# Rope's half swap in an attention stage: GpSimd's products replaced by transfers between partitions and one VectorE product

## The chip, the core and the metric

The kernel runs on one core of one Trainium2 chip. The metric is the device time of one execution in microseconds (us), the median of three runs. TensorE (PE) multiplies matrices, VectorE (DVE), ScalarE (ACT) and GpSimd (POOL) work on tiles of up to 128 partitions, SyncE (SP) issues the transfers of the weights.

## What is computed

Two transformer layers with expert lookup and one hybrid block on 256 tokens of width 1024, in float32. The change lies in the first layer's attention alone: eight heads, each with two query and key maps of width 64 whose softmaxes are subtracted. Its part of the reference:

```python
def _rope(t, cos, sin):
    half = t.shape[-1] // 2
    rot = jnp.concatenate([-t[..., half:], t[..., :half]], axis=-1)
    return (t * cos[None, :, None, :] + rot * sin[None, :, None, :]).astype(t.dtype)
...
    q = _rope(q.reshape(B, S, 2 * DIFF_HEADS, DIFF_HEAD_DIM), cos, sin)
    k = _rope(k.reshape(B, S, 2 * DIFF_HEADS, DIFF_HEAD_DIM), cos, sin)
...
    scale = DIFF_HEAD_DIM ** -0.5
...
        s = jnp.einsum('bhmqd,bhmkd->bhmqk', qblk, kh).astype(jnp.float32) * scale
        p = jax.nn.softmax(jnp.where(mask, s, -jnp.inf), axis=-1)
        a = p[:, :, 0] - lam * p[:, :, 1]
        return jnp.einsum('bhqk,bhkd->bhqd', a.astype(vh.dtype), vh)
```

## The kernel before

Every weight is streamed from memory in tiles of 128 × 1024 (`Stream`, lines 36 to 85): SP loads a tile raw, ACT copies it to hi (line 66), DVE subtracts it to lo (line 67), and a product becomes three matmuls, with hi, with lo, and with the low part of the activations (lines 157 to 159). There are four raw buffers and three pairs of parts; splits run two tiles ahead of use.

`layer0` (line 366) does the first layer's attention. `proj_half` (line 209) makes the first half of v, then `qk_head` (line 509) makes q and k of one head after the other: a projection (`proj_t`, 24 matmuls of 256 columns), `rope`, a tick. At the end come the second half of v, the output projection (`proj_n`) and the layer norm.

q and k of a head stand transposed: 128 partitions are two maps of 64, each two halves of 32, and the 256 tokens are the columns. `rope` (line 408) copies the projection from PSUM to z (ACT, line 414), multiplies it by cos to mc (DVE, line 415), makes the swapped products on POOL, four of 32 partitions, each reading another 32 partitions than it writes (line 418), and, one step later, adds both to r on DVE (line 420).

The order on each engine is the order in which the program is written; nothing is rescheduled. `Background` (line 88) lets a list of generators take one step at each tick, and there is a tick after each projection and each quarter of v. The generator `chunk` (line 503) of a head takes the two sums r in its first step and its scores (line 423, eight small matmuls) in its third, and adds the generator `head` (line 438). That has as steps: the mask and the maxima on DVE (lines 446 to 449), the exponentials p on ACT (line 453), the factors, p and aa on DVE (lines 463 to 469), transposes on TensorE (line 474), a copy ast, the product with v (lines 484, 485), a mean square, of, and the split oh, ol. The scores and the output projection share four PSUM banks, so that projection begins when the last head's p is done (line 526).

Of the kernel before, what the change touches and what calls it, by code (L numbers as in the profile page):

```python
# [9 lines left out]
F32 = mybir.dt.float32  # L10
# [5 lines left out]
ALU = mybir.AluOpType  # L16
AX = mybir.AxisListType

P = 128
D = 1024  # L20
T = 256
# [14 lines left out]
class Stream:  # L36
# [34 lines left out]
    def next(self):  # L71

        i = self.used
        self.used += 1
        self.load(i + 1 + self.ahead)
        self.split(i + 1 + self.split_ahead + self.extra, i)
        got = self.cut[i]
        self.cut[i] = None
        return got
# [46 lines left out]
class Kernel:  # L126
# [239 lines left out]
    def layer0(self, pool_x):  # L366
        nc, tc, a = self.nc, self.tc, self.a
        with ExitStack() as ctx:
            one = ctx.enter_context(tc.tile_pool(name="l0", bufs=1))
# [14 lines left out]
            sin = one.tile([P, T], F32, tag="sin", name="sin0")  # L384
            nc.sync.dma_start(cos, a["c_cos"])
            nc.sync.dma_start(sin, a["c_sin"])
            ones = one.tile([P, P], F32, tag="ones", name="ones0")
            nc.gpsimd.memset(ones, 1.0 / P)
            lp = one.tile([P, 4, 64], F32, tag="lp", name="lp0")
# [15 lines left out]
            v = self.jd  # L405
            halves, past, done = set(), set(), set()

            def rope(o, n):

                z = two.tile([P, T], F32, tag="z", name=f"z{n}")  # L410
                sw = two.tile([P, T], F32, tag="sw", name=f"sw{n}", bufs=4)
                mc = two.tile([P, T], F32, tag="mc", name=f"mc{n}", bufs=4)
                r = two.tile([P, T], F32, tag="rr", name=f"rr{n}", bufs=4)
                nc.scalar.copy(z, o)
                nc.vector.tensor_tensor(mc, o, cos, ALU.mult)
                for q in range(4):
                    to, src = slice(32 * q, 32 * q + 32), slice(32 * (q ^ 1), 32 * (q ^ 1) + 32)
                    nc.gpsimd.tensor_tensor(sw[to], z[src], sin[src], ALU.mult)  # L418
                yield
                nc.vector.tensor_tensor(r, mc, sw, ALU.add)  # L420
                yield r

            def scores(q, k):
# [14 lines left out]
            def head(h, s):  # L438
                blocks = (slice(0, P), slice(P, 3 * P))
                p = two.tile([P, 2, 3 * P], F32, tag="p", name=f"p{h}", bufs=3)  # L440
                aa = two.tile([P, 3, P], F32, tag="aa", name=f"aa{h}", bufs=3)
                mx = two.tile([P, 2, 2], F32, tag="mx", name=f"mx{h}", bufs=4)
                sm = two.tile([P, 2, 2], F32, tag="sm", name=f"sm{h}", bufs=4)
                for m in range(2):
                    late = s[m][:64, 64:448].rearrange("p (a b) -> p a b", b=64)[:, 0:5:4]
                    nc.vector.memset(late, NEG)
                    for qb in range(NB):
                        nc.vector.tensor_reduce(mx[:, qb, m : m + 1], s[m][:, blocks[qb]], AX.X, ALU.max)
                nc.vector.tensor_scalar(mx, mx, -0.125, None, ALU.mult)
                yield  # L450
                for m in range(2):
                    for qb in range(NB):
                        nc.scalar.activation(
                            p[:, m, blocks[qb]],
                            s[m][:, blocks[qb]],
                            AF.Exp,
                            bias=mx[:, qb, m : m + 1],
                            scale=0.125,
                            accum_out=sm[:, qb, m : m + 1],
                        )  # L460
                past.add(h)
                yield
                nc.vector.reciprocal(sm, sm)
                nc.vector.tensor_scalar(sm[:, :, 1], sm[:, :, 1], lam, None, ALU.mult)
                af = aa.rearrange("p a b -> p (a b)")
                for qb in range(NB):
                    c = blocks[qb]
                    nc.vector.tensor_scalar(p[:, 1, c], p[:, 1, c], sm[:, qb, 1:2], None, ALU.mult)
                    nc.vector.scalar_tensor_tensor(af[:, c], p[:, 0, c], sm[:, qb, 0:1], p[:, 1, c], ALU.mult, ALU.subtract)  # L469
                yield  # L470
                yield from self.bg.two_banks()
                at = self.ps("m")
                for i in range(3):
                    nc.tensor.transpose(at[:, i * P : i * P + P], aa[:, i], self.ident)
                yield
                ast = two.tile([P, 3 * P], F32, tag="ast", name=f"ast{h}", bufs=6)
                nc.scalar.copy(ast, at[:, : 3 * P])
                yield
                while h // 4 not in halves:
                    yield  # L480
                yield from self.bg.two_banks()
                o = self.ps("m")[:, :T]
                dv = slice(h * P, h * P + P)
                nc.tensor.matmul(o, v[:, 0, dv], ast[:, :T], start=True, stop=False)
                nc.tensor.matmul(o[:, P:T], v[:, 1, dv], ast[:, T:], start=False, stop=True)
                sq = two.tile([P, T], F32, tag="sq", name=f"sq{h}", bufs=4)
                of = two.tile([P, T], F32, tag="of", name=f"of{h}", bufs=4)
                nc.scalar.activation(sq, o, AF.Square)
                nc.scalar.copy(of, o)
                yield  # L490
                yield from self.bg.two_banks()
                ms = self.ps("m")[:, :T]
                nc.tensor.matmul(ms, ones, sq, start=True, stop=True)
                yield
                rs = two.tile([P, T], F32, tag="rs", name=f"rs{h}")
                nc.scalar.activation(rs, ms, AF.Ln, bias=self.eps[1e-5])
                nc.scalar.activation(rs, rs, AF.Exp, scale=-0.5)
                nc.vector.scalar_tensor_tensor(of, of, gcol, rs, ALU.mult, ALU.mult)
                yield
                self.part(oh[:, h], ol[:, h], of)  # L500
                done.add(h)

            def chunk(h, parts):
                q, k = (next(r) for r in parts)
                yield
                yield
                self.bg.add(head(h, scores(q, k)))

            def qk_head(h):
                parts = []  # L510
                for i in "qk":
                    parts.append(rope(self.proj_t(self.xh, self.xl), f"{i}0{h}"))
                    next(parts[-1])
                    self.bg.tick()
                self.bg.add(chunk(h, parts))
# [761 lines left out]
def layout(i):  # L1277

    f = np.float32
    r = {}  # L1280
# [21 lines left out]
    inv = (f(10000.0) ** (-np.arange(0, 64, 2, dtype=f) / f(64))).astype(f)  # L1302
    ang = (pos[:, None] * inv[None, :]).astype(f)
    r["c_cos"] = np.ascontiguousarray(np.tile(np.cos(ang).T, (4, 1))).astype(f)
    r["c_sin"] = np.ascontiguousarray(np.concatenate([np.sin(ang).T, -np.sin(ang).T] * 2)).astype(f)
    r["c_ident"] = np.eye(P, dtype=f)
    r["c_iota"] = np.tile(np.arange(P).reshape(1, P), (P, 1)).astype(np.float16)
    r["c_iotak"] = np.tile(np.repeat(np.arange(16), 8).reshape(1, 16, 8), (P, 1, 1)).astype(np.float16)
# [48 lines left out]
```

## Time and profile before

| | us |
|---|---|
| median of three runs | 2309.69 (2308.02 to 2313.12) |
| the profiled execution, its own time | 2311.31 |
| its span, first to last instruction | 2309.2 |
| PE busy in the span | 2230.4 (97%) |
| DVE busy | 1752.8 (76%) |
| ACT busy | 1237.7 (54%) |
| POOL busy | 58.3 (3%), 64 products and some fills |

The span is what the trace shows, and the time of the execution is 2.1 us more. A busy share is a mean over all stages: the attention stage of the first layer is the first 146 us of the span. Idle time of an engine counts only where another waits for it.

### The profile page before, as it was taken

The numbers are of one execution on the slowest core, as the hardware profiler recorded it, in microseconds if no ns is written. First come the engines' busy times: TensorE is split into PE (matmuls) and PEld (weight loads), VectorE is DVE, ScalarE is ACT, GpSimd is POOL, SyncE is SP. The second block draws the span as 40 slices with busy tenths as digits, with TensorE's granted clock in tenths as the row PEclk, the third lists the DMA queues.
The fourth block names the chain that finished last, engine by engine and source line by source line (L and its number), as shares of the span: only waits on it lengthen the run. The fifth ranks groups of instructions, "written<-read, shape, count | busy, mean of one in ns | idle before, by whom it ended". The sixth has DMA issues, their size and how long they took to land.

```text
span 2309.2 us, 39787 instructions
## 1 busy us (share of the span) xinstructions
PE 2230.4 (97%) x15028; PEld 2011.0 (87%) x15028; DVE 1752.8 (76%) x3488; ACT 1237.7 (54%) x2128; POOL 58.3 (3%) x79
## 2 busy tenths in 40 slices
PE   7889999999999999999999999999999899998998
PEld 6769999999888888887999999888888779997987
DVE  5968999888766767576998988766666856676754
ACT  4545454666555444584445566655444546755543
POOL 5400000000000000000000000000000000000000
PEclk9999999999999999999999999999999999999999
DMA  6336667555777777545666655677777564464764
GB/s 209 120 129 226 226 228 241 191 200 203 259 241 259 241 245 252 167 132 179 229 228 229 226 191 201 234 241 243 258 244 249 199 194 149 137 206 142 227 195 142
DMA packets 150657, 479.85 MB, mean 208 GB/s; under 512 B 17728, under 2 KB 18624, under 8 KB 149184
## 3 DMA queue, kind: packets, MB, share of 16 engines
q1 hardware_dynamic: 131456, 442.69, 59.1%
q10 hardware_dynamic: 19008, 34.61, 4.0%
q8 instruction: 118, 1.93, 0.3%
q14 instruction: 75, 0.61, 0.1%
HBM read 437.39 MB, written 39.85 MB: 207 GB/s over the span
## 4 chain that ended last, share of the span: by engine, by line
PE 85%; DVE 6%; ACT 4%; DMA 2%; issue 2%; POOL 1%; SPq 0%; DVEq 0%; ACTq 0%; POOLq 0%
PE ps_acc L182 34%; PE ps_h L157 15%; PE ps_h L159 14%; PE ps_h L158 14%; DVE lo L67 2%; PE ps_acc L805 1%; PE ps_acc L806 1%; ACT hi L66 1%; PE ps_acc L158 1%; PE ps_acc L159 1%; PE ps_acc L157 1%; DMA raw<-w_up 1%; PE ps_acc L689 0%; DVE aa L469 0%; POOL swq L418 0%
## 5 line engine op out<-in xcount | busy, mean ns | idle before, releaser
L67 DVE TENSOR_TENSOR lo<-raw,hi 128x1024 fp32r<-128x1024 f32 x740 | 904.9, 1226 | 454.2 <-ACT hi L66 451.8
L66 ACT CAST hi<-raw 128x1024 fp32r<-128x1024 f32 x740 | 775.4, 1050 | 437.3 <-issue 308.6
L157 PE MATMUL ps_h<-xh,hi 128*128 128x256 f32 x2784 | 790.3, 284 | 5.0 <-ACT r L1237 2.2
L159 PE MATMUL ps_h<-xh,lo 128*128 128x256 f32 x2784 | 774.3, 278 | 1.3 <-DVE lo L67 1.1
L158 PE MATMUL ps_h<-xl,hi 128*128 128x256 f32 x2784 | 774.4, 278 | 0.0
L157 PEld LDWEIGHTS ps_h<-xh,hi 128*128 128x128 f32 x2784 | 526.5, 189 | 11.8 <-ACT r L1237 2.4
L159 PEld LDWEIGHTS ps_h<-xh,lo 128*128 128x128 f32 x2784 | 525.1, 189 | 2.3 <-DVE lo L67 2.3
L158 PEld LDWEIGHTS ps_h<-xl,hi 128*128 128x128 f32 x2784 | 525.3, 189 | 0.2
L182 PE MATMUL ps_acc<-hi,wh 128*128 128x512 f32 x1024 | 315.4, 389 | 3.3 <-ACT wh L163 3.3
L182 PE MATMUL ps_acc<-hi,wo 128*128 128x512 f32 x1024 | 315.4, 389 | 0.0
L182 PE MATMUL ps_acc<-lo,wh 128*128 128x512 f32 x1024 | 315.1, 389 | 0.0
L832 ACT ACTIVATE hs<-ps_h 128x256 f32<-128x256 f32 x256 | 98.3, 384 | 344.1 <-PE ps_h L159 176.2
L182 PEld LDWEIGHTS ps_acc<-hi,wh 128*128 128x128 f32 x1024 | 192.1, 188 | 43.5 <-ACT wh L163 3.6
L182 PEld LDWEIGHTS ps_acc<-hi,wo 128*128 128x128 f32 x1024 | 192.3, 188 | 39.9
L182 PEld LDWEIGHTS ps_acc<-lo,wh 128*128 128x128 f32 x1024 | 192.3, 188 | 39.7
L164 DVE TENSOR_TENSOR wo<-jd,wh 128x256 fp32r<-128x256 f32 x256 | 107.2, 419 | 2.0 <-ACT wh L163 2.0
L856 DVE TENSOR_TENSOR jd<-G,jd 128x256 f32<-128x256 f32 x256 | 106.9, 418 | 2.2 <-ACT G L808 2.2
L163 ACT CAST wh<-jd 128x256 fp32r<-128x256 f32 x256 | 101.7, 397 | 10.4 <-DVE jd L856 10.4
L808 ACT ACTIVATE G<-ps_acc 128x64 f32<-128x64 f32 (+1 forms) x256 | 82.0, 385 | 6.6 <-PE ps_acc L806 1.0
L157 PE MATMUL ps_h<-hi,xh 128*128 128x512 f32 x160 | 70.8, 442 | 11.8 <-ACT hi L66 9.8
L158 PE MATMUL ps_h<-lo,xh 128*128 128x512 f32 x160 | 67.9, 424 | 5.7 <-DVE lo L67 5.7
L159 PE MATMUL ps_h<-hi,xl 128*128 128x512 f32 x160 | 68.0, 425 | 2.5 <-DVE xl L164 2.5
(323 smaller groups left out, 2384.3 us busy)
## 6 DMA issues: line engine op xcount, KB each, us to landing
raw<-peer_u SPq DMA_DIRECT2D x256, 512.0 KB, 4.5
raw<-peer_v SPq DMA_DIRECT2D x256, 512.0 KB, 4.3
H<-hs SPq DMA_DIRECT2D x128, 256.0 KB, 2.1
jd<-H ACTq DMA_DIRECT2D x128, 256.0 KB, 4.2
raw<-w_in SPq DMA_DIRECT2D x32, 512.0 KB, 3.7
raw<-w_up SPq DMA_DIRECT2D x32, 512.0 KB, 4.4
raw<-w_down SPq DMA_DIRECT2D x32, 512.0 KB, 3.7
raw<-w_qkv SPq DMA_DIRECT2D x24, 512.0 KB, 4.5
```

The lines of the kernel that those rows point to most:

```text
L66: self.nc.scalar.copy(hi, raw)
L67: self.nc.vector.tensor_sub(lo, raw, hi)
L157: mm(out, lh, rh, start=start, stop=False)
L158: mm(out, lh, rl, start=False, stop=False)
L159: mm(out, ll, rh, start=False, stop=stop)
L163: self.nc.scalar.copy(hi, src)
L164: self.nc.vector.tensor_sub(lo, src, hi)
L182: mm(acc[half], x, w[:, half * 512 : half * 512 + 512], start=a, stop=b)
L805: mm(out, o[:, 0, j], o[:, 1, j], start=True, stop=False)
L808: nc.scalar.activation(gt[:, :, 4 * g : 4 * g + 4], ps.rearrange("p (t i) -> p i t", t=4)[:, first:end], AF.Copy, scale=1.0 / GSCALE,)
L832: nc.scalar.activation(hs[i // 2][:, i % 2], o, AF.Gelu)
L856: nc.vector.tensor_tensor(w, g[:, i - first], hl[i // 2][:, i % 2], ALU.mult)
```

## The change

`rope` no longer multiplies on POOL. Four transfers, issued from POOL's queue, bring the other 32 partitions of z into a new tile zs, and DVE multiplies zs by sin in one operation of 128 partitions. The signs in the table of sin change place accordingly. z has four buffers instead of two. `chunk` has one step more at its start, so that a head's sums, and all that follows from them, come one tick later. The factor 1/8 of the scores goes into two tables for q, made once by POOL, and the maxima are taken negated, so that the scaling operation on them and the scale of the exponential go.

```diff
+            cosq, sinq = (one.tile([P, T], F32, tag=t, name=t + "0") for t in ("cosq", "sinq"))
+            nc.gpsimd.tensor_scalar(cosq, cos, 0.125, None, ALU.mult)
+            nc.gpsimd.tensor_scalar(sinq, sin, 0.125, None, ALU.mult)
...
-            def rope(o, n):
+            def rope(o, n, cos, sin):
 
-                z = two.tile([P, T], F32, tag="z", name=f"z{n}")
-                sw = two.tile([P, T], F32, tag="sw", name=f"sw{n}", bufs=4)
+                z = two.tile([P, T], F32, tag="z", name=f"z{n}", bufs=4)
+                zs = two.tile([P, T], F32, tag="zs", name=f"zs{n}", bufs=4)
                 mc = two.tile([P, T], F32, tag="mc", name=f"mc{n}", bufs=4)
                 r = two.tile([P, T], F32, tag="rr", name=f"rr{n}", bufs=4)
                 nc.scalar.copy(z, o)
                 nc.vector.tensor_tensor(mc, o, cos, ALU.mult)
                 for q in range(4):
-                    to, src = slice(32 * q, 32 * q + 32), slice(32 * (q ^ 1), 32 * (q ^ 1) + 32)
-                    nc.gpsimd.tensor_tensor(sw[to], z[src], sin[src], ALU.mult)
-                yield
-                nc.vector.tensor_tensor(r, mc, sw, ALU.add)
+                    nc.gpsimd.dma_start(zs[32 * q : 32 * q + 32], z[32 * (q ^ 1) : 32 * (q ^ 1) + 32])
+                yield
+                nc.vector.tensor_tensor(zs, zs, sin, ALU.mult)
+                nc.vector.tensor_tensor(r, mc, zs, ALU.add)
                 yield r
...
-                        nc.vector.tensor_reduce(mx[:, qb, m : m + 1], s[m][:, blocks[qb]], AX.X, ALU.max)
-                nc.vector.tensor_scalar(mx, mx, -0.125, None, ALU.mult)
+                        nc.vector.tensor_reduce(mx[:, qb, m : m + 1], s[m][:, blocks[qb]], AX.X, ALU.max, negate=True)
...
                             bias=mx[:, qb, m : m + 1],
-                            scale=0.125,
...
             def chunk(h, parts):
+                yield
                 q, k = (next(r) for r in parts)
                 yield
                 yield
...
-                    parts.append(rope(self.proj_t(self.xh, self.xl), f"{i}0{h}"))
+                    parts.append(rope(self.proj_t(self.xh, self.xl), f"{i}0{h}", *((cosq, sinq) if i == "q" else (cos, sin))))
...
-    r["c_sin"] = np.ascontiguousarray(np.concatenate([np.sin(ang).T, -np.sin(ang).T] * 2)).astype(f)
+    r["c_sin"] = np.ascontiguousarray(np.concatenate([-np.sin(ang).T, np.sin(ang).T] * 2)).astype(f)
```

DVE's order where the projections of head 5 end. In the names, mcq05 is mc of q of head 5, rrq04 the sum r of q of head 4, lo17 the low part of the 18th weight tile; the first piece is before, the second the change.

```order
L415 TENSOR_TENSOR mcq05_744<-ps_h20_717,cos0_115 128x256
L420 TENSOR_TENSOR rrq04_628<-mcq04_627,swq04_626 128x256
L420 TENSOR_TENSOR rrk04_685<-mck04_684,swk04_683 128x256
L67 TENSOR_TENSOR lo17_778<-raw17_711,hi17_777 128x1024
L415 TENSOR_TENSOR mck05_808<-ps_h25_781,cos0_115 128x256
L463 RECIPROCAL sm2_703<-sm2_703 128x4
```

```order
L67 TENSOR_TENSOR lo17_764<-raw17_702,hi17_763 128x1024
L418 TENSOR_TENSOR mck05_794<-ps_h21_767,cos0_115 128x256
L422 TENSOR_TENSOR zsq04_618<-zsq04_618,sinq0_120 128x256
L423 TENSOR_TENSOR rrq04_620<-mcq04_619,zsq04_618 128x256
L422 TENSOR_TENSOR zsk04_675<-zsk04_675,sin0_116 128x256
L423 TENSOR_TENSOR rrk04_677<-mck04_676,zsk04_675 128x256
L67 TENSOR_TENSOR lo18_830<-raw18_761,hi18_829 128x1024
```

The sums of head 4 stood behind mc of head 5's q, ahead of lo17; now they stand behind mc of its k, ahead of lo18, each behind its product.

DVE's order at the last rope sum, before and in the change:

```order
L420 TENSOR_TENSOR rrk07_1071<-mck07_1070,swk07_1069 128x256
L67 TENSOR_TENSOR lo23_1151<-raw23_1103,hi23_1150 128x1024
L164 TENSOR_TENSOR ol0_136<-of2_1018,oh0_135 128x256
L463 RECIPROCAL sm5_1093<-sm5_1093 128x4
L464 TENSOR_SCALAR sm5_1093<-sm5_1093,lam0_128 128x2
```

```order
L67 TENSOR_TENSOR lo23_1136<-raw23_1093,hi23_1135 128x1024
L499 SCALAR_TENSOR_TENSOR of2_1070<-of2_1070,gcol0_127,rs2_1151 128x256
L422 TENSOR_TENSOR zsq07_990<-zsq07_990,sinq0_120 128x256
L423 TENSOR_TENSOR rrq07_992<-mcq07_991,zsq07_990 128x256
L422 TENSOR_TENSOR zsk07_1053<-zsk07_1053,sin0_116 128x256
L423 TENSOR_TENSOR rrk07_1055<-mck07_1054,zsk07_1053 128x256
L67 TENSOR_TENSOR lo24_1183<-raw24_1133,hi24_1182 128x1024
L164 TENSOR_TENSOR ol0_140<-of2_1070,oh0_139 128x256
L464 RECIPROCAL sm5_1126<-sm5_1126 128x4
```

lo23, the last tile of v, stood behind the last sum and now stands ahead of it; the softmax of head 5 follows in both.

POOL's order at the first ropes, before and in the change:

```order
L388 MEMSET ones0_119 128x128
L418 ISA
L418 TENSOR_TENSOR swq00_248<-zq00_247,sin0_116 32x256 x4
L418 TENSOR_TENSOR swk00_289<-zk00_288,sin0_116 32x256 x4
L418 TENSOR_TENSOR swq01_330<-zq01_329,sin0_116 32x256 x4
```

```order
L388 ISA
L388 TENSOR_SCALAR cosq0_119<-cos0_115 128x256
L389 TENSOR_SCALAR sinq0_120<-sin0_116 128x256
L391 MEMSET ones0_123 128x128
L420 DMA zsq00_252<-zq00_251 32x256 x4
L420 DMA zsk00_293<-zk00_292 32x256 x4
```

Four products for each rope have become four transfers in the same place, 64 in all, and the two table products stand ahead of them.

## Rows read from the trace of the kernel before

**Rows 1.** Windows: stretch, its length, each engine's busy us (instructions); clock, DMA share, GB/s.
```profile
24.00:44.00 20.00, 19.93 (x175) 19.04 (x173) 12.20 (x15) 7.98 (x13) 16.84 (x18) 1.00 0.50 155
...
83.00:94.00 11.00, 9.60 (x77) 8.61 (x77) 10.27 (x22) 6.20 (x19) 5.99 (x8) 1.00 0.33 96
...
200.00:300.00 100.00, 100.00 (x881) 98.62 (x880) 96.70 (x306) 46.97 (x76) 0.00 (x0) 1.00 0.68 226
```

**Rows 2.** Waits from 15 to 150 us: who waited for whom, us in total, times, longest.
```profile
ACT zq L414 <- POOL swq L418: 9.8, 3, 3.9
...
DVE rrk L420 <- POOL swk L418: 5.8, 3, 2.2
```

**Rows 3.** Timeline of POOL: start, us, engine, line, operation, count, idle before it.
```profile
42.87 4.22 POOL L418 TENSOR_TENSOR swq<-zq,sin 32x256 f32<-32x256 f32 x4
...
51.42 4.18 POOL L418 TENSOR_TENSOR swq<-zq,sin 32x256 f32<-32x256 f32 x4
...
85.11 3.20 POOL L418 TENSOR_TENSOR swk<-zk,sin 32x256 f32<-32x256 f32 x4 [4.26 <-ACT zk L414]
```

**Rows 4.** Groups of DVE by form, 44 to 98.5 us: busy us, mean ns.
```profile
L468 DVE TENSOR_SCALAR p<-p,sm 128x128 f32<-128x128 f32 x5 | 3.9, 783 | 0.2
...
L468 DVE TENSOR_SCALAR p<-p,sm 128x256 f32<-128x256 f32 x4 | 3.5, 864 | 0.0
```

**Rows 5.** The same groups from 98.5 to 135 us.
```profile
L468 DVE TENSOR_SCALAR p<-p,sm 128x256 f32<-128x256 f32 x4 | 1.4, 346 | 0.0
...
L468 DVE TENSOR_SCALAR p<-p,sm 128x128 f32<-128x128 f32 x3 | 0.9, 285 | 0.1
```

**Rows 6.** Timeline of DVE, 82 to 118 us.
```profile
82.65 0.41 DVE L420 TENSOR_TENSOR rrq<-mcq,swq 128x256 f32<-128x256 f32 x1
...
93.85 0.42 DVE L420 TENSOR_TENSOR rrq<-mcq,swq 128x256 f32<-128x256 f32 x1
...
101.78 1.23 DVE L67 TENSOR_TENSOR lo<-raw,hi 128x1024 fp32r<-128x1024 f32 x1
102.92 0.48 DVE L498 SCALAR_TENSOR_TENSOR of<-of,gcol,rs 128x256 f32<-128x256 f32 x1
103.32 0.42 DVE L420 TENSOR_TENSOR rrq<-mcq,swq 128x256 f32<-128x256 f32 x1
103.65 0.42 DVE L420 TENSOR_TENSOR rrk<-mck,swk 128x256 f32<-128x256 f32 x1
104.56 1.22 DVE L67 TENSOR_TENSOR lo<-raw,hi 128x1024 fp32r<-128x1024 f32 x1 [0.49 <-ACT hi L66]
...
106.04 0.17 DVE L463 RECIPROCAL sm<-sm 128x4 f32<-128x4 f32 x1
...
107.98 0.17 DVE L446 MEMSET ps_acc<- 64x128 f32 x1
...
109.67 0.17 DVE L449 TENSOR_SCALAR mx<-mx 128x4 f32<-128x4 f32 x1
...
112.56 1.22 DVE L67 TENSOR_TENSOR lo<-raw,hi 128x1024 fp32r<-128x1024 f32 x1 [0.83 <-ACT hi L66]
...
117.82 0.17 DVE L449 TENSOR_SCALAR mx<-mx 128x4 f32<-128x4 f32 x1
```

**Rows 7.** Single lines: duration ns min/median/max; DMA issues: count, KB, us to landing.
```profile
L823 SPq DMA_DIRECT2D H<-hs x128: 326/327/328, 186.2 to 1477.1; - x128
...
L418 POOL TENSOR_TENSOR swq<-zq,sin x32: 712/733/1692, 26.1 to 90.8; 32x256 f32<-32x256 f32 x32
...
ident<-c_ident SPq DMA_DIRECT2D x1, 64.0 KB, 3.0
```

**Rows 8.** Groups of POOL over the whole span: busy us, mean ns.
```profile
L418 POOL TENSOR_TENSOR swq<-zq,sin 32x256 f32<-32x256 f32 x32 | 29.8, 930 | 27.0 <-ACT zq L414 25.1
```

**Rows 9.** Timeline of ACT at the first two copies z.
```profile
25.65 0.37 ACT L414 COPY zq<-ps_h 128x256 f32<-128x256 f32 x1 [1.44 <-PE ps_h L159]
...
28.37 0.37 ACT L414 COPY zk<-ps_h 128x256 f32<-128x256 f32 x1 [1.40 <-PE ps_h L159]
```

## The prediction

> **What bounds the kernel now.** I read the busy times by stretch first, because the kernel is 2309 us long and the change touches one stage. From 200 us on TensorE is busy for every microsecond of the stretch, while between 24 and 44 us and between 83 and 94 us it is not, and there VectorE (DVE) or GpSimd (POOL) is full [rows 1]. The only POOL arithmetic of the program, 64 small products, lies between 26 and 99 us; so all that the change can move lies in the first 120 us, and what it wins or loses there shifts everything behind it.
>
> Inside the stage there are two regimes. The waits show ScalarE's copy z standing 9.8 us for POOL's products of q (z has two buffers) and DVE's sum standing 5.8 us for POOL [rows 2]: in the beginning POOL is the pace. Its timeline says so: the products of one projection take 4.2 us, those of one head (q and k) start 8.55 us apart (42.87 to 51.42), with no gap. Later it has gaps, 4.26 us before 85.11, waiting for ScalarE's copy [rows 3]; there DVE is the pace, with 10.27 of 11 us busy [rows 1]. The DVE groups tell why it is so slow: the product of p with its factor costs 783 ns for 128 columns and 864 ns for 256 while POOL works, against 285 and 346 ns from 98.5 us on, when POOL is done [rows 4, 5]. So POOL's products slow DVE as well as making it wait.
>
> **The change part by part, against the profiled execution** (2311.3 us, span 2309.2; the median of the three runs is 1.6 us below it, and I subtract the sum from the median). The mark I follow is the end of the last rope sum, rrk of head 7: 103.65 + 0.42 = 104.1 us [rows 6].
>
> *Taken off DVE.* All POOL products go, hence the slowness of what ran beside them. DVE's work for a head, once undisturbed, is read from starts in the stretch without POOL [rows 6]: two splits lo at 1.14 (101.78 to 102.92), of 0.40 (102.92 to 103.32), reciprocal to aa 1.94 (106.04 to 107.98), memsets and maxima 1.69 (107.98 to 109.67), rope operations 0.33 each (103.32 to 103.65) and ol, of the same shape, as much. The negation of the maxima (0.17 to 0.47 us) goes into the reductions; nothing in the trace prices a negated reduction, and I take the same 0.29 and 0.41 us; between nothing more and 0.2 us each it would be up to 0.8 us a head.
>
> *Added to DVE.* A product zs by sin for each of q and k: a second input in place of POOL's, the same shape as the rope sum, 0.33 from start to start. So each head has six rope operations, 2.0. Sum for a head: 2.28 + 2.0 + 0.40 + 0.33 + 1.94 + 1.69 = 8.64, with something for waits 8.7 us. Before, the same mark returned after 11.2 us (82.65 to 93.85). Each zs now waits for four transfers; waits that are over when reached cost little, and no row prices them.
>
> *Added to POOL: 64 transfers, 8 a head, and two table products.* This is the price on which all hangs, and no row has it. Bounds: SyncE issues a transfer in 0.33 us (the stores of H, 128 times); POOL's slowest product took 1.69 us [rows 7]. The nearest row is POOL's own instruction on the same 32 × 256 slice, 0.93 us in the mean [rows 8]. I take 1.0 us, that row rounded towards the middle of the bounds. For the way from issue to landing I take 3.0 us, the 64 KB load of the identity, nearest in size [rows 7]; 2 to 4 us would shift the first head by 1 us and no pace. [...] The two table products (q's eighth of cos and sin, once) have the time until the first z at 25.65 [rows 9], which POOL now spends idle; with that cover gone they would cost what POOL's slowest product costs per slice, under 4 us once.
>
> *Moved.* The rope sums of a head come one tick, one projection, later in DVE's order, and so its scores on TensorE; z, and the new zs, have four buffers. So ScalarE's copy no longer waits for POOL, and a transfer has a whole projection more to land: that is what hides 4 × 1.0 + 3.0 us. Late next is zs of k, at whose wait DVE holds up the next split lo, and with it TensorE.
>
> *Sum.* The first z is there at 26.0 (25.65 + 0.37), the second projection follows 2.72 later [rows 9]; so TensorE alone would give a head every 5.5. Eight transfers: the last is issued at 26.0 + 7 × 1.0 = 33.0, lands at 36.0, four rope operations on DVE, 37.3. POOL sets the pace at 8.0 a head until DVE has the softmax of the first heads to do, through head 3: 37.3 + 3 × 8.0 = 61.3. Then DVE sets it: 61.3 + 4 × 8.7 = 96.1. That is **8.0 us before 104.1**.
>
> *The end of the stage.* In the order before, three splits lie between the last rope sum and the last maximum, with waits of 0.49 and 0.83 us for hi; that took from 104.1 to 118.0 (117.82 + 0.17), 13.9 us [rows 6]. In the new order it is two splits (the third comes ahead), of once, ol twice and twice the 3.63 us of softmax and maxima, 2.28 + 0.40 + 0.66 + 7.26 = 10.6, and some 0.7 of waiting for ScalarE's p: 11.3. **2.6 us less.** The tick that the last scores come later costs nothing here, since TensorE has its second half of v done and waits for p either way. Behind that the order is nearly the same, and I count nothing. Together 10.6 us: 2309.7 − 10.6 = **2299.1 us**.
>
> **The rivals.**
>
> *The transfers are cheap (0.73 us or less, chance 0.20).* For: the fastest POOL product is 0.71 us [rows 7], and a transfer multiplies nothing. Then POOL is never the pace. DVE reaches the first sums after the fourth projection (25.65 + 3 × 2.72 = 33.8) and is done at 35.7; TensorE allows 5.5 us for the next head, DVE 6.0 for the one after (two lo, six rope operations, one set of maxima: 2.28 + 2.0 + 1.69), 7.9 for two more (with the softmax, 1.94), 8.3 (with of) and twice 8.7 for the rest. The mark is at 88.7, and with the 2.6 the gain is 18.0: 2292 us.
>
> *Small DVE operations stay slow (0.17).* Rows 4 and 5 show that these two engines stand in each other's way, not which access does it. If issuing a transfer holds what POOL's product held, the two products p stay at their present means, (783 − 285) + (864 − 346) = 1.0 us a head more, and POOL loses their 0.6 us, 8.6 a head, which is still under DVE's: mark at 61.3 + 4 × 9.7 = 100.1, gain 4.0 + 2.6 = 6.6, 2303 us, and less where other operations share in it. [...]
>
> *POOL becomes the bound (0.23).* One mechanism: 8 transfers a head must be issued in order, on one engine, and DVE waits for each four of them. The mark is then 26.0 + 7c + 3.0 + 1.3 + 56c = 30.3 + 63c. Above c = 1.09 us POOL is slower than DVE's 8.7 in every head; at 106.7 (104.1 + 2.6), that is c = 1.21, the gain is gone. At 1.4 it is 118.5, 11.8 us slower: 2321 us; at the bound of 1.69, 30 us slower. For it: even the simple product took up to 1.69 us beside DVE. Against: its median is 0.73 [rows 7].
>
> *It does nothing (0.04).* The tables and the order say that POOL's products are gone, so only a stage that something else paces could stay; the waits in rows 2 speak against it.
>
> **How the numbers follow.** Forecast 0.36, for prices between 0.75 and 1.14 us; the rivals as given. About 0.2% (4.6 us) is what a measurement of this kernel can tell from no change. Faster by more: 0.36 + 0.20 + half of the port case = 0.64. Within: the other half (0.09), the case of nothing (0.04) and 0.02 of the POOL case = 0.15. Slower: 0.21. The range goes from the cheap case, 2291, to a price of about 1.38 us, 2320; what lies above is about one chance in ten, and some remains below.
>
> **What would show it.** POOL's issues in the new trace: their spacing is the price c; near 1.0 the first rope sums end near 37 us, and the last near 96. [...] DVE's waits should name the transfers into zs in the first heads only; if they do in all, POOL is the bound. A zs product of more than 0.45 us, or a reduction longer than now, would break the sum of 8.7. And the distance from the last rope sum to the last maximum should be about 11.3 us; if that grows instead, the extra tick was not free. Wrong altogether is the prediction if the stage ends later than 146 us in the new trace.

## The result, and the profile after

The changed kernel took 2293.31 us (median of 6 runs, 2289.42 to 2295.97) against 2309.0 us of the kernel before (6 runs, 2308.0 to 2315.5): a ratio of 0.9925, with a 95% interval of 0.991 to 0.994. That is faster by 0.75%, some 16 us where 10.6 were forecast. The profiled execution took 2293.14 us (span 2291.4).

The windows of the changed kernel are those of [rows 1]: stretch, its length, each engine's busy us (instructions), clock, DMA share, GB/s.

```profile
24.00:44.00 20.00, 20.00 (x177) 19.54 (x176) 14.62 (x26) 9.25 (x14) 13.13 (x27) 1.00 0.80 232
83.00:94.00 11.00, 11.00 (x61) 8.55 (x59) 10.45 (x30) 7.16 (x19) 0.00 (x0) 1.00 0.71 238
200.00:300.00 100.00, 100.00 (x880) 98.75 (x879) 96.63 (x311) 46.58 (x74) 0.00 (x0) 1.00 0.68 227
```

Behind 200 us nothing has moved. In the attention stage TensorE is now full in both stretches, and POOL is done before 83 us. POOL's line 420 (the transfers) gives the price on which the forecast hung: duration in ns, minimum, median and maximum, and the way to landing.

```profile
L420 POOL DMA_DIRECT2D zsq<-zq x32: 496/496/683, 25.5 to 74.3; - x32
L420 POOL DMA_DIRECT2D zsk<-zk x32: 496/496/498, 28.2 to 77.5; - x32
...
DMA to landing us min/median/max: 1.7/3.1/5.3
```

A transfer costs POOL 0.50 us, half of the forecast's 1.0; it lands 3.1 us after, as assumed. The waits of the changed kernel from 15 to 150 us (us in total, times, longest) answer to [rows 2]:

```profile
POOL zsq L420 <- ACT zq L417: 26.5, 8, 12.6
...
ACT zk L417 <- PE ps_h L159: 10.9, 8, 1.6
ACT zq L417 <- PE ps_h L159: 10.1, 8, 2.5
...
ACT p L455 <- DVE mx L451: 0.8, 2, 0.5
```

Nobody waits for POOL any more, and VectorE waits for no transfer. The copy z stands for TensorE's projection alone, and POOL stands for the copy. The last line will matter below. Before, in the same window, ScalarE's exponentials stood 18.8 us for the maxima:

```profile
ACT p L453 <- DVE mx L449: 18.8, 7, 3.7
```

VectorE's groups from 44 to 98.5 us (busy us, mean ns | idle before) answer to [rows 4]:

```profile
L451 DVE TENSOR_REDUCE mx<-ps_acc 128x1 f32<-128x256 f32 x13 | 5.4, 414 | 0.0
L451 DVE TENSOR_REDUCE mx<-ps_acc 128x1 f32<-128x128 f32 x13 | 3.8, 291 | 0.4
...
L422 DVE TENSOR_TENSOR zsq<-zsq,sinq 128x256 f32<-128x256 f32 x6 | 2.5, 417 | 0.0
...
L469 DVE TENSOR_SCALAR p<-p,sm 128x256 f32<-128x256 f32 x7 | 2.4, 347 | 0.0
...
L469 DVE TENSOR_SCALAR p<-p,sm 128x128 f32<-128x128 f32 x7 | 2.0, 286 | 0.2
```

p costs 286 and 347 ns, the values that [rows 5] had when POOL was done. A negated maximum costs 291 and 414 ns for 128 and 256 columns, and a plain one cost 290 and 414 in the same window before. Last, VectorE's timeline of the changed kernel at the marks that the forecast followed, as in [rows 6]:

```profile
34.93 0.42 DVE L423 TENSOR_TENSOR rrk<-mck,zsk 128x256 f32<-128x256 f32 x1
...
80.96 0.43 DVE L423 TENSOR_TENSOR rrk<-mck,zsk 128x256 f32<-128x256 f32 x1
...
89.21 0.43 DVE L423 TENSOR_TENSOR rrk<-mck,zsk 128x256 f32<-128x256 f32 x1
...
99.95 0.62 DVE L451 TENSOR_REDUCE mx<-ps_acc 128x1 f32<-128x128 f32 x2
...
125.47 1.28 DVE L305 SCALAR_TENSOR_TENSOR lny<-x,ps_acc 128x512 f32<-128x512 f32 x2
```

The first operation of the layer norm (lny) starts at 125.47 us; before, it started at 145.09:

```profile
145.09 1.28 DVE L305 SCALAR_TENSOR_TENSOR lny<-x,ps_acc 128x512 f32<-128x512 f32 x2
```

So the stage became 19.6 us shorter, and the two profiled executions differ by 2311.31 − 2293.14 = 18.2. I use lny as the finest mark for all runs. What follows it is the same program in each, and took 2162.7 to 2171.9 us in the profiles of all fourteen kernels: 9.2 us of spread that follows none of the edits, and which the totals carry too. The marks have a smaller spread of their own: the first copy z, which stands ahead of the first swap, starts between 24.52 and 26.20 us, at 25.65 before and at 24.78 in the change. So 0.9 of the 19.6 us lie ahead of the swap, and 18.75 us behind it.

### The profile page after: what moved, and what is told of

It is laid out like the page before. It is cut to its first block, busy times and chain, and to the rows that moved or that the text cites. A ratio compares the mean times of both kernels' runs of the same rounds, so it can differ in the third digit from the quotient of the medians.

```text
span 2291.4 us, 39855 instructions
## 1 busy us (share of the span) xinstructions
PE 2224.8 (97%) x15028; PEld 2007.0 (88%) x15028; DVE 1744.0 (76%) x3496; ACT 1238.1 (54%) x2128; POOL 35.6 (2%) x81
## 4 chain that ended last, share of the span: by engine, by line
PE 87%; DVE 5%; ACT 4%; DMA 2%; issue 2%; POOL 0%; SPq 0%; DVEq 0%; ACTq 0%
PE ps_acc L182 35%; PE ps_h L157 15%; PE ps_h L159 15%; PE ps_h L158 14%; DVE lo L67 2%; PE ps_acc L807 1%; PE ps_acc L808 1%; ACT hi L66 1%; PE ps_acc L158 1%; PE ps_acc L157 1%; PE ps_acc L159 1%; DMA raw<-w_up 1%; PE ps_acc L691 0%; PE ps_m L289 0%; DVE lns L308 0%
```

## The experiments

Each kernel was compared with the kernel before on its own chip, where that one's median was 2309 to 2313 us; so ratios, not times, are compared between the kernels. The marks are those of each profile, in us; a maximum ends with its reduction, without the negation that follows it where there is one.

| kernel | ratio to before, 95% interval | first rope sum ends | last rope sum ends | last maximum ends | lny starts |
|---|---|---|---|---|---|
| before | 1 | 34.69 | 104.07 | 117.78 | 145.09 |
| the change | 0.9925 (0.991 to 0.994) | 35.35 | 89.64 | 100.57 | 125.47 |
| negation and tables alone | 0.9982 (0.9973 to 0.9991) | 34.39 | 102.25 | 114.90 | 139.60 |
| tick and z's buffers alone | 0.9988 (0.9978 to 0.9998) | 35.32 | 103.23 | 115.44 | 142.44 |
| both of these, products kept | 0.9973 (0.9963 to 0.9983) | 36.82 | 102.25 | 114.90 | 139.77 |
| change without the tick | 0.9919 (0.9906 to 0.9932) | 34.02 | 88.86 | 101.39 | 126.48 |
| eight transfers a projection | 0.9965 (0.9952 to 0.9979) | 37.96 | 98.44 | 109.39 | 133.73 |
| sixteen transfers | 1.0267 (1.0251 to 1.0282) | 44.09 | 168.02 | 178.95 | 203.56 |
| two products beside | 0.9964 (0.995 to 0.9977) | 35.87 | 100.97 | 111.91 | 136.32 |
| ScalarE's queue | 1.0039 (1.0025 to 1.0052) | 41.17 | 113.90 | 126.63 | 151.42 |
| ScalarE's queue, products beside | 1.0039 (1.0025 to 1.0052) | 42.00 | 113.67 | 127.61 | 152.40 |
| p on ScalarE | 0.9925 (0.9912 to 0.9938) | 35.65 | 89.56 | 100.80 | 126.62 |
| one transfer, p on ScalarE | 0.9914 (0.9901 to 0.9928) | 35.22 | 88.92 | 100.16 | 125.22 |
| no product by the sine | 0.9899 (0.988 to 0.9918) | 34.26 | 86.30 | 98.49 | 122.85 |

### The parts alone

Negated maxima and q's tables, in the kernel before:

```diff
...
-    ... nc.vector.tensor_reduce(mx[...], s[m][:, blocks[qb]], AX.X, ALU.max)
-nc.vector.tensor_scalar(mx, mx, -0.125, None, ALU.mult)
+    ... nc.vector.tensor_reduce(mx[...], s[m][:, blocks[qb]], AX.X, ALU.max, negate=True)
...
```

> The kernel before with only the negated maxima and q's tables with the eighth in them; POOL's products stay. Theory (this part frees VectorE of its small negation, 0.17 to 0.47 us a head, in the five heads that VectorE paces): 1 to 2 us less than before, 2307 us, and reductions of the same 0.29 and 0.41 us. Rival (VectorE's small operations are not what paces those heads, POOL is): no difference, 2308.5 to 2310 us. Second rival (a negated reduction costs more): reductions longer by up to 0.2 us and no gain or a loss of up to 4 us.

The extra tick and four buffers of z, in the kernel before:

```diff
-z = two.tile([P, T], F32, tag="z", name=f"z{n}")
+z = two.tile([P, T], F32, tag="z", name=f"z{n}", bufs=4)
...
 def chunk(h, parts):
+    yield
     q, k = (next(r) for r in parts)
```

> The kernel before with only the extra tick and four buffers of z; POOL's products stay. Theory (the gain is POOL's arithmetic gone: its 4.2 us a projection and the slowing of VectorE beside it): the waits of ScalarE and VectorE for POOL go (9.8, 5.1 and 5.8 us), but POOL still sets 8.5 us a head in the beginning, p stays near 800 ns, and the program gains at most 3 us: 2306 to 2309 us. Rival (the gain is that the sums are asked for later and z has room, and products on POOL would have done as well): 2301 us or less, with the last rope sum under 98 us.

Both of them together, so that only POOL's products and the plain sum remain of the kernel before:

> The change with only its main part undone: POOL's four products a projection and the plain rope sum stay as in the kernel before, while the extra tick, z's four buffers, the negated maxima and q's tables are those of the change. Theory (POOL's products off the engine are worth most of the gain, the small parts add up beside it): the two small parts alone gave 0.18 and 0.12 per cent, together 7 us, so 2303 to 2307 us; p stays at some 780 and 860 ns; the last rope sum ends near 101 us, and what is left to the change, 9 to 13 us, is the swap's. Rival (with the small parts the products are no longer in the way): 2297 us or less. Second rival (the small parts win the same time twice): 2308 to 2311 us.

The first gave 0.18% (4.2 us), more than twice what was expected, the second 0.12%, and together 0.27%, near their sum, though the intervals would also allow that the second adds nothing to the first. At lny both together come no earlier than the first alone (139.77 and 139.60 us), but their first z came 1.1 us later (26.20 and 25.07). Reckoned from the first z to lny, the gains are 4.9, 1.8 and 5.9 us. In the last kernel the swap, undone, is missing: 0.9973 against 0.9925, some 11 us, and at lny 139.77 − 125.47 = 14.3 us, or 12.9 from the first z. So the swap's move off POOL is the larger part, with about two thirds of the gain. With POOL's products kept, the tick and the buffers take away ScalarE's waits for POOL, but VectorE's stay (the last line below), POOL stays slow and VectorE beside it too. These are VectorE's groups from 44 to 90 us of the kernel with products kept:

```profile
L67 DVE TENSOR_TENSOR lo<-raw,hi 128x1024 fp32r<-128x1024 f32 x9 | 14.4, 1604 | 0.0
...
L469 DVE TENSOR_SCALAR p<-p,sm 128x256 f32<-128x256 f32 x4 | 3.5, 864 | 0.0
...
L423 DVE TENSOR_TENSOR rrk<-mck,swk 128x256 f32<-128x256 f32 x5 | 3.2, 633 | 5.2 <-POOL swk L421 5.2
```

Why the negation alone is worth more than its own time is seen on ScalarE at the last head. Before, one operation of VectorE over all four maxima came last (from 117.82 to 117.99 us), and the first exponential could start only then:

```profile
118.02 0.37 ACT L453 ACTIVATE p<-ps_acc,mx 128x128 f32<-128x128 f32 x1 [2.18 <-DVE mx L449]
```

In the changed kernel it starts when the maxima of the first map are there, while VectorE still takes those of the second (until 100.57 us):

```profile
99.77 0.37 ACT L455 ACTIVATE p<-ps_acc,mx 128x128 f32<-128x128 f32 x1
```

The last exponential's sum is then read 0.95 us after the last maximum (101.32 + 0.20 − 100.57), before 1.96 us (119.53 + 0.21 − 117.78). The run with the negation alone has the same 0.96 us (115.66 + 0.20 − 114.90), so it is this part that does it. It does more than that for TensorE, as is shown further down at the step behind the last maximum.

### The extra tick

```diff
 def chunk(h, parts):
-    yield
     q, k = (next(r) for r in parts)
```

> The change without its extra tick; all else as in it. Theory (the tick is what hides the transfers): a transfer of k is issued by POOL in 0.5 us after ScalarE's copy and lands about 3 us after that, four of them some 4.5 us after the copy, while a projection takes 2.7 us in the beginning; so VectorE now stands at the product of zs for 1.5 to 3 us in each of the first three heads and up to 1 us in the later ones, the last rope sum comes 4 to 8 us later than 89.6, and the program takes 2297 to 2303 us. Rival (VectorE has enough other work, so the tick does nothing): 2291 to 2295 us, the last rope sum within 1.5 us of 89.6. Second rival (the tick costs, since the last scores come a projection later): 2288 to 2291 us.

The ratio is that of the change, within the intervals. VectorE does wait for zs of k, 1.31, 1.30 and 0.83 us in the first three heads, near what the first theory said, and not at all later:

```profile
DVE zsk L422 <- DMA zsk<-zk: 3.5, 3, 1.3
```

But the sums, asked for one projection earlier, end 1.3 us earlier (34.02), so that nothing is lost. At the end the tick gives something back: without it the last maximum comes 12.5 us behind the last rope sum (101.39 − 88.86), with it 10.9, and lny starts 1.0 us later (126.48 for 125.47), which the totals can't show. The rival holds in the total, and the tick isn't needed to hide the transfers.

### The price of a transfer

Each transfer halved, and, in a second kernel in the same way, cut into four (sixteen of 8 partitions, the edit not shown):

```diff
-for q in range(4):
-    nc.gpsimd.dma_start(zs[32 * q : 32 * q + 32], z[32 * (q ^ 1) : 32 * (q ^ 1) + 32])
+for q in range(8):
+    c = 16 * q ^ 32
+    nc.gpsimd.dma_start(zs[16 * q : 16 * q + 16], z[c : c + 16])
```

> The change with each transfer halved (16 partitions, eight a projection), so that POOL pays per projection what the forecast had put on four at 1.0 us. Theory (the forecast's sum was right but for the price, 0.50 in place of 1.0): POOL issues in 0.5 us each, 8 us a head; the first rope sums end near 37 instead of 35.4, the last one at 92 to 96 instead of 89.6, and the time is 2296 to 2300 us. Rival (TensorE with 8.1 us a head is the bound anyway, and eight issues of 0.5 us fit beside it): the last rope sum within 2 us of 89.6, 2292 to 2296 us.

> The change with each transfer cut into four (8 partitions, sixteen a projection). Theory (a transfer's price on POOL is by its number, about 0.5 us, whatever its size): POOL is the bound at 16 us a head, the last rope sum comes at 26 + 128 x 2 x 0.5 + 4 = 158 us, 68 us late, the time near 2360 us, and the waits name the transfers in all heads. Rival (the price is by rows moved, so a quarter of the size costs a quarter): at 0.12 to 0.2 us each, no difference from the change.

POOL's transfers of the kernel with eight (16 partitions each), and of that with sixteen (8 partitions):

```profile
L421 POOL DMA_DIRECT2D zsq<-zq x64: 487/487/674, 25.3 to 87.5; - x64
```
```profile
L421 POOL DMA_DIRECT2D zsq<-zq x128: 521/521/717, 25.2 to 153.2; - x128
```

The price goes by the number of transfers, not by their size: 496 ns each in the median for 32 partitions, 487 for 16 and 521 for 8. With eight, POOL pays per projection what the forecast had put on four, and the forecast's own rhythm appears: it had rope sums ending at 37.3, 45.3, 53.3, 61.3, 70.0, 78.7, 87.4 and 96.1; here they end at 37.96, 46.87, 54.17, 62.25, 71.92, 80.41, 89.21 and 98.44. The ratio of 0.9965 is 2300.9 us on 2309.0, near the forecast's 2299.1. With sixteen POOL is the bound at 17.7 us a head ((168.02 − 44.09) / 7), and VectorE's waits from 24 to 175 us name the transfers in all eight heads:

```profile
DVE zsk L423 <- DMA zsk<-zk: 56.9, 8, 9.0
```

The last rope sum came 10 us later than expected: an issue takes 0.521 us there, so 16.7 a head (32 × 0.521) in place of 16, and to it come POOL's own short waits, some 9 us in all besides the first. TensorE's granted clock was lower too in that kernel (0.74 in the mean from 24 to 175 us, with TensorE busy in 89.1 of 151 us; in the change 0.98, with 142.3 busy).

### Products beside, and ScalarE's queue

Two former products a projection behind the four transfers, into a tile that nobody reads (the tile itself, and one buffer less of the copied maps, are not shown):

```diff
...
     nc.gpsimd.dma_start(zs[32 * q : 32 * q + 32], z[32 * (q ^ 1) : 32 * (q ^ 1) + 32])
+for q in range(2):
+    nc.gpsimd.tensor_tensor(sw[to], z[src], sin[src], ALU.mult)
```

> The change with its four transfers a projection and, behind them on POOL, two of the former products into a tile that nobody reads (one buffer of the copied maps less, for room). POOL is as full as with eight transfers a projection (4 x 0.50 + 2 x 0.73 to 0.93 = 3.5 to 3.9 us, there 3.9), but half of it is arithmetic. Theory (POOL's arithmetic slows VectorE, its issuing doesn't): p, aa and the splits are longer, p between 350 and 800 ns, VectorE's head grows by 1 us or more over the 8.1 us that TensorE allows, and the last rope sum comes 5 to 10 us after 89.6, the end at 2297 to 2304 us, although the transfers come first and so land earlier than with eight. Rival (only POOL's time counts): VectorE's operations at 285, 350 and 1220 ns, the time no later than with eight transfers and the last rope sum at 90 to 95 us.

The ratio is that of eight transfers, so the totals don't tell the theories apart. The last rope sum came at 100.97 us, 11.3 behind the change's: later than the theory's 5 to 10 and than the rival's 90 to 95. The trace shows the slowing: VectorE's groups from 44 to 90 us are

```profile
L455 DVE TENSOR_REDUCE mx<-ps_acc 128x1 f32<-128x256 f32 x10 | 4.1, 414 | 0.0
L426 DVE TENSOR_TENSOR zsk<-zsk,sin 128x256 f32<-128x256 f32 x5 | 3.4, 672 | 3.8 <-DMA zsk<-zk 3.8
...
L473 DVE TENSOR_SCALAR p<-p,sm 128x128 f32<-128x128 f32 x4 | 2.6, 651 | 0.1
...
L419 DVE TENSOR_TENSOR mcq<-ps_h,cosq 128x256 f32<-128x256 f32 x5 | 2.1, 415 | 1.6 <-ACT zq L418 1.6
```

p with 128 columns takes 651 ns in place of 286, zs of k 672 in place of 419. With aa of 128 columns (576 for 352), rrk (672 for 426), zsq (464 for 417) and two splits (1297 for 1218), all means of the same window in the two kernels, that is 0.37 + 0.25 + 0.22 + 0.25 + 0.05 + 0.16 = 1.3 us a head. At lny it is 2.6 us behind the kernel with eight transfers; but POOL needed 3.5 to 4.4 us a projection here, there 3.8 to 4.0 and short waits of its own, so how much of this is VectorE's slowness and how much POOL's pace stays open.

The other attempt was to take the transfers off POOL, as a base on which its products could be put back with nobody waiting:

```diff
-nc.gpsimd.dma_start(zs[...], z[...])
+nc.scalar.dma_start(zs[...], z[...])
```

> The change with its 64 transfers issued by ScalarE, right behind its copy z, in place of POOL. Theory (the transfers are far from the path: POOL issued one in 0.50 us, four a projection, and TensorE and VectorE are both full at some 8.1 us a head): no difference from the change, 2291 to 2296 us. Rival (an issue on ScalarE costs what one of SyncE did, 0.33 us, so 2.6 us a head on an engine with 5 to 7 of 8 to 9 us busy; its exponentials come later): 2296 to 2304 us. It is also the base for the next run.

> As the run with ScalarE's queue, but POOL again makes the four products a projection of the kernel before, into a tile that nobody reads (one buffer of the copied maps less, for room); they change no result and nobody waits for them except the copy z, for its fourth buffer back. Theory (POOL's arithmetic beside VectorE is what cost the time, whoever waits for it): p with 128 columns near 780 ns and with 256 near 860 as before, aa near 800 to 880, the splits up to 1.36 us; VectorE's head grows from 8.0 to 10 us or more, the last rope sum comes 8 to 14 us later than in the run with ScalarE's queue, and so does the end: 2301 to 2308 us. Rival (the wait of the rope sums for POOL was the cost, and with nobody waiting the products are free): within 2 us of that run, the last rope sum under 92 us.

The first alone made the kernel slower than before, by 0.39%, and slower than the change by 26 us at lny. These are ScalarE's line, the way to landing, and ScalarE's timeline:

```profile
L420 ACTq DMA_DIRECT2D zsq<-zq x32: 514/602/1128, 26.1 to 96.5; - x32
...
DMA to landing us min/median/max: 1.8/1.9/4.9
```
```profile
37.89 0.37 ACT L417 COPY zk<-ps_h 128x256 f32<-128x256 f32 x1
38.29 2.44 ACTq L420 DMA_DIRECT2D zsk<-zk  x4
40.77 1.05 ACT L66 CAST hi<-raw 128x1024 fp32r<-128x1024 f32 x1 [2.51 <-DMA zsk<-zk]
```

An issue takes 0.60 us there, not the 0.33 of SyncE's stores [rows 7]; four a projection hold up the cast hi by 2.5 us. VectorE's next split waits for hi (23.1 us in all from 24 to 110 us), and the product mc, for which TensorE's next projection waits, stands behind that split: the first two heads come 7.7 us apart instead of 5.4. In the chain of work followed back from 60 to 24 us these issues are 40% of the time. Later TensorE's granted clock is also lower there (0.72 from 60 to 72 us and 0.69 from 83 to 94, in the change 1.00 in both); what part of the 26 us that is, no run separates. The transfers themselves land sooner (1.9 us after the issue in the median, 3.1 from POOL), but in the kernel the issuing engine's time decided: four take 2.44 us of ScalarE, for whose hi VectorE then waits, against 1.96 of POOL.

The second has the same ratio, so POOL's products cost nothing on top that the totals show (1.0 us at lny). My theory's 8 to 14 us didn't come, but the base was no base: with ScalarE as the pace, a slower VectorE is hidden. That it was slower is plain, in the same groups from 44 to 90 us:

```profile
L67 DVE TENSOR_TENSOR lo<-raw,hi 128x1024 fp32r<-128x1024 f32 x9 | 13.3, 1481 | 1.3 <-ACT hi L66 1.3
...
L473 DVE TENSOR_SCALAR p<-p,sm 128x256 f32<-128x256 f32 x3 | 2.6, 859 | 0.0
...
L419 DVE TENSOR_TENSOR mcq<-ps_h,cosq 128x256 f32<-128x256 f32 x4 | 1.7, 416 | 0.2 <-ACT zq L418 0.2
```

### What paces the heads now

The product of p on ScalarE; then this with a single transfer a projection, which copies z and leaves out the swap; then the change without the product by the sine. The last two don't compute the kernel's result.

```diff
-nc.vector.tensor_scalar(p[:, 1, c], p[:, 1, c], sm[:, qb, 1:2], None, ALU.mult)
+nc.scalar.mul(p[:, 1, c], p[:, 1, c], sm[:, qb, 1:2])
```
```diff
-for q in range(4):
-    nc.gpsimd.dma_start(zs[32 * q : 32 * q + 32], z[32 * (q ^ 1) : 32 * (q ^ 1) + 32])
+nc.gpsimd.dma_start(zs, z)
```
```diff
-nc.vector.tensor_tensor(zs, zs, sin, ALU.mult)
```

> The change with the product of p and its factor (two operations a head, 0.32 and 0.38 us from start to start on VectorE) done by ScalarE instead. Theory (VectorE alone paces the heads, at 8.0 to 8.8 us each, with no idle time between 53 and 96 us): six heads each 0.6 to 0.7 us shorter, the last rope sum near 86 us and 2289 to 2290 us in all. Rival (TensorE, 11.0 of 11 us busy from 83 to 94 us, is the next bound, or the way from VectorE to ScalarE and back costs as much as is saved): 2292 to 2297 us, with VectorE idle at aa for ScalarE's p.

> The change with one transfer a projection in place of four, a plain copy of z: the swap of the halves is left out, so the scores are not the reference's. The product of p is on ScalarE as in the run before that had it. So POOL and VectorE are both relieved, POOL to 1 us a head and VectorE to 7.4. Theory (from 48 us on TensorE, with some 8.1 us of matmuls a head, is the bound, and nothing cheaper on POOL or VectorE can help): 2290 to 2295 us, heads still 8.0 to 8.8 us apart, the last rope sum at 88 to 90. Rival (VectorE and the landing of the transfers hold it by turns, so relieving one alone, as before, could not show): heads near 7.5 us apart, the last rope sum at 84 to 86, 2286 to 2289 us.

> The change without the product of zs and the sine: the rope sums add the swapped halves unmultiplied, so the scores are not the reference's. It takes 0.45 us from start to start twice a head off VectorE, 0.9 us of 8.0 to 8.8, and puts no handover in its place (with p on ScalarE, VectorE stood 0.53 us a head at aa for it, which gave most of the 0.70 us back). Theory (TensorE, with hardly a gap from 48 to 81 us, is a bound of its own at some 8 us a head): heads stay 7.8 us apart or more, the last rope sum at 87 to 90, the time 2290 to 2295 us. Rival (VectorE alone paces the heads, and TensorE only looks full): heads 7.1 to 7.9 us apart, the last rope sum at 84 to 85.5, the time 2287 to 2289.5 us.

The first changed nothing, and VectorE's waits from 44 to 92 us say why: it stands half a microsecond in each head for what it gave away, so 0.70 us taken off left some 0.17.

```profile
DVE aa L470 <- ACT p L469: 3.2, 6, 0.5
```

The second has the same wait, so it doesn't tell TensorE and VectorE apart, though it does show that POOL, with one transfer in place of four, isn't the limit any more. The third takes 0.9 us a head off VectorE with no handover, and falls between the theories (the last rope sum at 86.30 us, where one said 87 to 90 and the other 84 to 85.5): from the third head to the eighth the change needs 41.9 us (47.73 to 89.64), this kernel 39.7 (46.63 to 86.30), so 0.45 us a head came through, half of what was taken off. So VectorE is the pace in the changed kernel, and something else stands less than half a microsecond behind it, at 7.9 us a head. These are VectorE's wait of this kernel from 46 to 87 us, and two of its windows:

```profile
DVE lo L67 <- ACT hi L66: 2.0, 3, 1.0
```
```profile
44.00:60.00 16.00, 16.00 (x137) 14.33 (x136) 14.46 (x39) 10.53 (x31) 9.69 (x21) 1.00 0.60 171
60.00:72.00 12.00, 11.81 (x96) 10.96 (x95) 10.96 (x26) 8.61 (x26) 4.87 (x10) 1.00 0.57 172
```

Of the 4.5 us taken off in five heads 2.2 came through, and 2.0 of the other 2.3 are VectorE's waits for ScalarE's hi. ScalarE itself stands 8.6 us in that time for TensorE's projections (zk 5.1, zq 3.5), and TensorE is busy in 16.00 of 16 us from 44 us on and in 11.81 of the next 12. So I take TensorE to be what stands behind. No run relieved it, and none tested the rival, the order of ScalarE's work with hi behind z and the exponentials: this is argued and not shown. The stage ended 2.6 us sooner; between the ratios 0.9899 and 0.9925 the intervals overlap. No version that computes the same was faster than the change.

## Why the prediction was right, and where its size was off

The direction, the place and the mechanism were right; the size was 5 us short of the medians. Step by step, in the profiled executions:

- **What bounds.** Right. With POOL's products gone its waits [rows 2] are gone, p went back to 286 and 347 ns, and nothing behind 200 us changed. One thing went with them that the forecast didn't have: from 44 to 83 us TensorE's granted clock was 0.87 in the mean before, with 29.4 of 39 us busy, and 1.00 in the change, with 37.6. What this is worth by itself no run separates.
- **VectorE's 8.7 us a head.** Right, and 0.3 too long. With no wait of VectorE in its timeline between 53 and 96 us, heads came 8.0 to 8.8 us apart, 8.39 in the mean of the last four (56.08 to 89.64), so 1.2 us of the 6.4 by which the mark below came early are this term's. A wait that was over when reached cost nothing that shows: zs of q starts 0.33 us after the mc ahead of it (45.73 to 46.06). The added product took 0.42 us and the negated maxima nothing more.
- **The price of a transfer.** This is the term that was mis-sized: "I take 1.0 us, that row rounded towards the middle of the bounds". It is 0.50 us. The nearest row was of the wrong kind: [rows 8] is arithmetic of POOL beside VectorE, and 0.50 is nearer to SyncE's 0.33 [rows 7], an issue. So POOL, which the forecast let pace the first four heads at 8.0 us, needs 4.0 a head and paces none: the sum of head 3, forecast at 61.3 us, ended at 56.08, and these 5.2 us are the other part of the 6.4 (0.9 of them the earlier first z). VectorE's waits, which were to name the transfers in the first heads, name them in none. The upper bound was also misread, though nothing hangs on it: POOL's slowest product was one of k with 1.72 us, and 1.69 is the slowest of q.
- **The mark.** The last rope sum was forecast at 96.1 us and came at 89.6: 14.4 us gained, not 8.0. The rival of cheap transfers had 88.7, with the steps 35.7, then 5.5, 6.0, 7.9, 7.9, 8.3, 8.7 and 8.7; measured were 35.35, then 5.45, 6.93, 8.35, 8.04, 8.43, 8.84 and 8.25. So that rival, with a chance of 0.20, is what happened, and its 2292 us the better number. That its gain of 18.0 us meets the measured 18.2 is luck in part: its mark was a microsecond early, it too counted nothing behind the last maximum, and the rest of the program took 1.4 us more. The run with eight transfers is the forecast's own case.
- **The end of the stage.** Forecast 11.3 us from the last rope sum to the last maximum, measured 10.9 (100.57 − 89.64), for 13.9 before: 3.0 us gained where 2.6 were said.
- **Behind the last maximum** I counted nothing, and 2.2 us came: 24.9 us to lny (125.47 − 100.57), before 27.1 (145.09 − 117.99). It comes with the negated maxima, a step that was missed: with them alone the distance is 24.7 us (139.60 − 114.90), with the tick and buffers alone 26.8 (142.44 − 115.65, where the negation ends). Between the kernel before and the negation alone, the 2.4 us can be split. 0.8 us is the joint wait that went: ScalarE's last sum ends 1.75 us behind VectorE's last operation before (119.74 − 117.99), and 0.96 with the negation alone (115.86 − 114.90). 1.6 us is TensorE's clock. These are its rows behind the last maximum before, from its timeline and from a window in the form of [rows 1] (the third number from the end is the granted clock):

```profile
118.99 0.50 PE L182 MATMUL ps_acc<-hi,oh 128*128 128x512 f32 x1 [2.42 <-ACT p L453]
...
120.13 1.02 PE L182 MATMUL ps_acc<-lo,oh 128*128 128x512 f32 x2
...
124.01 0.62 PE L182 MATMUL ps_acc<-lo,oh 128*128 128x512 f32 x2
```
```profile
121.00:122.00 1.00, 1.00 (x4) 0.82 (x3) 1.00 (x2) 0.00 (x0) 0.00 (x0) 0.50 0.00 0
```

and with the negation alone:

```profile
115.07 0.49 PE L182 MATMUL ps_acc<-hi,oh 128*128 128x512 f32 x1 [1.39 <-ACT p L455]
...
116.25 0.63 PE L182 MATMUL ps_acc<-lo,oh 128*128 128x512 f32 x2
...
118.51 0.62 PE L182 MATMUL ps_acc<-lo,oh 128*128 128x512 f32 x2
```
```profile
116.00:120.00 4.00, 4.00 (x18) 3.31 (x19) 3.03 (x8) 3.35 (x6) 0.00 (x0) 1.00 0.26 40
```

Before, TensorE had stood 2.42 us for the exponentials, and soon after its granted clock was 0.50 (from 121 to 122 us; 0.56 in the mean from 120.13 to 124.01). With the negation alone it had stood 1.39 us, and the clock was 1.00 from 116 to 120 us. What lowered the clock no run separates. The same matmuls took 3.88 us (120.13 to 124.01) and 2.26 (116.25 to 118.51); from there to lny both kernels need 21.1 us. In the change the clock is 1.00 from 101.4 to 115 us; its own 2.2 us aren't split.
- **The sum.** 14.4 + 3.0 + 2.2 = 19.6 us; the rest of the program took 1.4 us more in this execution (2166.2 to 2167.7), inside the spread, and 18.2 remain.
- **The extra tick** was "what hides 4 × 1.0 + 3.0 us". At 0.50 us there is less to hide, and it is free but not needed.
- **The other rivals.** POOL as the bound is real, and sixteen transfers show it; 0.50 us lies far from the break-even of 1.21. The rival of small VectorE operations that stay slow (the port case of the chances) didn't come: p takes 286 and 347 ns, and POOL's issues took 0.496 us in the median and 0.683 at most beside a busy VectorE. What spreads the landing from 1.7 to 5.3 us, no run separates.

## What to carry to other kernels

Price a DMA issue by issues, by their number and by the engine that makes them: here 0.49 to 0.52 us on GpSimd for 8 to 32 partitions, and 0.60 on ScalarE for 32. Put small transfers on the engine that has nothing else to do, not on the one whose transfers land soonest (ScalarE here, with 1.9 us against 3.1); four a projection on ScalarE's queue cost 26 us that four on GpSimd didn't. And look for the small operation that joins results which were ready one by one: folding the negation into the reductions let the exponentials start half a head's maxima earlier, and TensorE, which waited 1.39 us for them in place of 2.42, had a granted clock of 1.00 there and not of 0.50.

## What was not expected of the hardware

POOL's arithmetic slowed only some operations of VectorE. With all four products a projection on POOL, those with both inputs in SBUF grew (splits from 1218 to as much as 1604 ns, zs of k from 419 to 632), and so did p, which has one such input and a factor per partition (256 columns from 347 to 859 and more). With two products a projection only some of them did: zs of k took 672 ns, but rrq stayed at 425 and p with 256 columns at 344. Those that read PSUM did not: mc stayed at 410 to 417 ns, the maxima at 290 to 292 and 413 to 415, in each kernel with products on POOL. Which access clashes with which, and why p slowed with one input in SBUF, no run here shows.
